# The second branch's gate columns early, as quads of blocks with seven products for eight, and gates kept in DRAM

## The chip, the cores and the metric

One core of a Trainium2 chip runs the program. TensorE (PE) multiplies, VectorE (DVE) and ScalarE (ACT) do elementwise work, GpSimd (POOL) does a few small steps, and SyncE (SP) issues almost all DMAs. The metric is the device time of one execution in microseconds (us), the median of several runs.

## The reference

One layer of an encoder on 256 tokens of 2048 features, all in float32. `w_in` has 8256 columns, the last 4096 of which are the gates of the two branches.

```python
h = rms_norm(x, g_mix)
proj = h @ w_in
c_q, c_kv, k_r, q_d, k_d, v_d, gate = jnp.split(proj, cuts, axis=-1)
...                                  # latent attention -> o_a, dilated attention -> o_b
y_a = o_a.reshape(B, S, MLA_HEADS * V_DIM) @ w_o_mla
y_b = o_b.reshape(B, S, dh) @ w_o_dil
g = jax.nn.sigmoid((gate + b_gate).astype(jnp.float32)).astype(x.dtype)
g = g.reshape(B, S, N_BRANCH, D_MODEL)
x = x + (g[:, :, 0] * y_a + g[:, :, 1] * y_b) @ w_o
gt, up = jnp.split(rms_norm(x, g_ffn) @ w_gate_up, 2, axis=-1)
return x + (jax.nn.silu(gt) * up) @ w_down
```

## The kernel before

**Products in three.** Every float32 operand is split into a rounded high part (a cast on ACT) and the rest (a subtraction on DVE); a product is three products of parts (`mm3`, L426): high by high, high by rest, rest by high. Activations are split once, weights as they stream in. The normalised x stands transposed in SBUF as `xT` (16 row blocks of 128 features by 256 tokens, high `xTh` and rest `xTl`). The division by the root mean square comes after the product, as a factor `rx` per token (`st["x"]`).

**Groups, chunks, steps.** The weight columns are cut into groups (L716 on). An ordinary group has up to 512 columns and accumulates over its row blocks in two banks of PSUM, one for each 128 tokens; its weights come in chunks of two row blocks (512 KB), and a step is the 12 products of a chunk. At the end of a group its `evac` function takes the sums out of PSUM. The groups run in this order: q latents, kv latents, then `g_b` (rotary key, dilated q, k, v) mixed with the up-projections of the latents, the first branch's gates (`evac_g0`, four groups), then the output projections of the two branches, between which the second branch's gates lie (`evac_g1`, four groups), then `w_o`, then the feed-forward part (FFN).

**Quads.** A feed-forward group has 1024 columns, 512 of the gate half and 512 of the other, and takes its 16 row blocks two at a time (`Quad`, L74). Two row blocks, two halves of the columns and two tiles of tokens make a 2x2 by 2x2 block product, which takes eight products of blocks, each over 512 columns. Quads 2, 4 and 6 of eight (`FAST`, L43) take seven products of sums of blocks instead (factors L869); the others are called plain. For these DVE adds weight blocks (L844 to L847) before they are cast and split, and differences of activation blocks are made by DVE (L628 to L631). The seven sums are held in seven PSUM banks, of the tiles mA, mB, sC and sD (`hold_banks`, L127), and are put together by DVE: five steps after the last seven-product quad (`evac_fast`, L658), four after the last plain one (start of `evac_pair`, L670).

**The stream.** SP issues the weight loads in the order of the chunks into three buffers `x` (`xp`, L100); the buffer comes free when its chunk is split. ACT casts and DVE subtracts up to three chunks ahead of PE into six buffers `wh`/`wl` (`wp`, L101). Attention runs as jobs (L431): a step of the main sequence is followed by at most one piece of a job. Loads of biases, residuals and tables are issued a number of steps ahead of a group (`at`, L932). Up to the last two groups ahead of the FFN the program stands in the order in which it is written (`in_order`, L106); after that a scheduler orders it.

**The start.** In the first group the tiles of x come in between the weights. PE transposes them, ACT makes `xTh` (L212), DVE `xTl` (L217). Squares of x are summed on ACT between the steps, and POOL makes `rx` from them.

Of the kernel before, what the change touches and what calls it, by code (L numbers as in the profile page):

```python
# [19 lines left out]
P = 128  # L20
# [21 lines left out]
NPAIR = KD // 2  # L42
FAST = (2, 4, 6)  # L43


# [21 lines left out]
class Group:  # L67
    def __init__(self, w, c0, n, ks, lhs, evac, needs=None, sizes=None):
        self.w, self.c0, self.n, self.ks = w, c0, n, ks
        self.lhs, self.evac, self.needs = lhs, evac, needs or {}  # L70
        self.sizes = sizes


class Quad:  # L74


    def __init__(self, group, i):
        self.group, self.i, self.fast = group, i, i in FAST
        plain = [k for k in range(NPAIR) if k not in FAST]
        self.first, self.last = i == plain[0], i == plain[-1]  # L80
        self.first_fast, self.last_fast = i == FAST[0], i == FAST[-1]

# [12 lines left out]
@with_exitstack  # L95
def layer_kernel(ctx: ExitStack, tc: tile.TileContext, a: dict, out: bass.AP):
    nc = tc.nc
# [141 lines left out]
    def transpose_in(act, k0, nk, src, gname=None):  # L239

        ps = side(f"tr_{act.name}{k0}").rearrange("p (k s) -> p k s", s=S)
        for k in range(nk):
            for t in range(NT):
                nc.tensor.transpose(ps[:, k, t * P:(t + 1) * P], src(t, k0 + k), ident)
        h, l = act.tiles(k0 // 4)
        o = k0 % 4
        if gname is None:
            split_evac((h[:, o:o + nk], l[:, o:o + nk], ps[:, :nk], None))
        else:
            split_evac(*((h[:, o + k], l[:, o + k], ps[:, k], gain(gname, k0 + k)) for k in range(nk)))  # L250

    xT = Act("xT", KD)

    def job_x(k0, nk):
        transpose_in(xT, k0, nk, lambda t, k: xn[k // 4][:, t, (k % 4) * P:(k % 4 + 1) * P], "g_mix")
        return
        yield

    xjobs, xjob_of = [], {}
# [292 lines left out]
    for p in range(4):  # L552
        attn["mla", p] = Job(job_attn("mla", p), [prep["kr"], gains])
        attn["dil", p] = Job(job_attn("dil", p), [prep["qd"], prep["kd"], bdone["vd"]])


    g0, tj, mT, gbias = {}, {}, Act("mT", KD), {}
# [14 lines left out]
    def evac_g0(j):  # L572
        def evac(ps, step):
            g0[j] = gate_evac(ps, j, f"g0_{j}")
        return evac

    def evac_ya(j):
        def evac(ps, step):
            nc.scalar.activation(g0[j], g0[j], AF.Sigmoid)
            nc.vector.tensor_mul(g0[j], ps, g0[j])  # L580
        return evac

    def evac_g1(j):
        def evac(ps, step):
            tj[j] = gate_evac(ps, 4 + j, f"g1_{j}")
            nc.scalar.activation(tj[j], tj[j], AF.Sigmoid)
        return evac
# [25 lines left out]
    def job_h(i):  # L613
# [7 lines left out]
        if i not in FAST:  # L621
            hP[i] = t4([P, 2, 2, S], f"hP{i}", F32R)
            split_evac(*((hP[i][:, 0, k], hP[i][:, 1, k], ps[:, k], g[k]) for k in range(2)))
        else:
            v, l, h = t4([P, 8, P], f"hs{i}"), t4([P, 7, P], f"hsl{i}", F32R), t4([P, 7, P], f"hsh{i}", F32R)
            nc.scalar.activation(v[:, 0:8:7], ps[:, 0].rearrange("p (t s) -> p t s", t=NT), AF.Copy, scale=g[0])
            nc.scalar.activation(v[:, 1:3], ps[:, 1].rearrange("p (t s) -> p t s", t=NT), AF.Copy, scale=g[1])
            nc.vector.tensor_sub(v[:, 3], v[:, 7], v[:, 2])  # L628
            nc.vector.tensor_sub(v[:, 4], v[:, 7], v[:, 0])
            nc.vector.tensor_sub(v[:, 5], v[:, 0], v[:, 3])  # L630
            nc.vector.tensor_sub(v[:, 6], v[:, 1], v[:, 5])  # L631
            split_pair(h, l, v[:, :7])
            hq[i] = (h, l)
        return
# [22 lines left out]

    def evac_fast(q):  # L658

        bank, z, u = held["q"], t4([P, NT, 512], f"z{q.group.c0}"), t4([P, NT, 512], f"u{q.group.c0}")  # L660
        add, sub = nc.vector.tensor_add, nc.vector.tensor_sub
        with tc.high_priority(offset=PRIO):
            nc.scalar.copy(u[:, 0], bank[1])
            sub(z[:, 0], bank[6], u[:, 0])
            add(u[:, 1], bank[7], z[:, 0])
            add(z[:, 1], bank[5], u[:, 1])
            add(z[:, 0], bank[5], z[:, 0])
        q.group.zu = z, u

    def evac_pair(half, i, last):  # L670

        def evac(zu, step):
            q = held["q"]
            z, u = zu
            add, sub = nc.vector.tensor_add, nc.vector.tensor_sub
            with tc.high_priority(offset=PRIO):
                add(z[:, 1], q[0], z[:, 1])
                add(z[:, 0], q[3], z[:, 0])
                add(u[:, 0], q[2], u[:, 0])  # L679
                sub(u[:, 1], q[4], u[:, 1])  # L680
            r = st["2"]
# [42 lines left out]

    g_in(0, 512, evac_lat("cq"), sizes=[1, 1])
    g_in(512, 512, evac_lat("ckv"))
# [6 lines left out]
    g_b(6)  # L733
    for j in range(4):
        g_in(OFF_GATE + 512 * j, 512, evac_g0(j))
# [84 lines left out]
    def load(c):  # L820
        g, gi, ks, q = chunks[c]
        t = xt[c] = xp.tile([P, 4, 512], F32, name=f"x{c}", tag="x")
        if q:
            for kk in range(2):
                src = g.w[(2 * q.i + kk) * P:(2 * q.i + kk + 1) * P].rearrange("p (n f) -> p n f", n=2)
                nc.sync.dma_start(t[:, 2 * kk:2 * kk + 2], src[:, :, g.c0:g.c0 + 512])
            return
# [22 lines left out]
    def split(c):  # L850
# [4 lines left out]
        h = w8(f"wh{c}")  # L855
        h, l = (h, w8(f"wl{c}")) if gi >= ffn_at else (h[:, :2], h[:, 2:])
        s = (slice(None), slice(0, 4 if q else len(ks)), slice(0, 512 if q else g.n))
# [14 lines left out]
    def products_quad(c):  # L872
        q = chunks[c][3]
        bank, w = held["q"], parts.pop(c)
        if not q.fast:
            h, l = w
            for t, n in ((1, 0), (0, 0), (0, 1), (1, 1)):
                m = PLAIN[t, n]
                for kk in range(2):
                    s = slice(t * P, (t + 1) * P)  # L880
                    mm3(bank[m], hP[q.i][:, 0, kk, s], hP[q.i][:, 1, kk, s], h[:, 2 * kk + n], l[:, 2 * kk + n],
                        q.first and kk == 0, q.last and kk == 1)
        else:
            h, l = hq[q.i]
            for m in (1, 6, 7, 5, 3, 2, 4):
# [89 lines left out]
    splits(2)  # L975
    jobs.extend((gains, xstat))
    gains.ready = 8
    xstat.ready = 2
    for i, (c, ks, first, last) in enumerate(steps):
        g, gi, allks, q = chunks[c]  # L980
        if first and gi == ffn_at - 2:
            in_order.close()
        for fn in early.get(i, ()):
            fn()
# [11 lines left out]
        if gi == ffn_at and not held:  # L996
            hold_banks()
        ps = products(i)
        if last and gi < len(groups) - 1:
# [60 lines left out]
```

## Time and profile before

| | |
|---|---|
| median of three runs | 1356.53 us (1354.4, 1356.53, 1360.9) |
| the profiled execution | 1356.11 us, span from first to last instruction 1354.3 us, granted clock 1.000 |
| PE, DVE, ACT, POOL busy | 99%, 70%, 48%, 3% of the span |
| DMA | 257.14 MB, mean 190 GB/s |
| gate groups of the second branch | between the output projections; the first output projection starts at 367 us, the last gate of the four is taken out of PSUM at 522 us |
| feed-forward part | from 634.7 us to the end |

A row of a group of instructions gives line, engine, operation, output<-inputs, shapes and count, then total busy us and mean ns of one, then the idle time of the engine ahead of them and what ended it. A row of a timeline starts with its start and duration in us; in square brackets stands an idle time before it. A row of a window gives the stretch and its length, then the busy us of PE, weight loads, DVE, ACT and POOL with their counts, the PE clock, the busy share of the DMA engines and GB/s. A row of waits gives who waited for whom: total us, times, longest. Matmuls overlap in the records, so their duration is longer than the distance of their starts; the distance is what a product costs.

### The profile page before, as it was taken

To read this page: it belongs to the slowest core of one execution; us is meant where nothing else is said; L and a number is where in the kernel's file an instruction comes from. 1 tells how busy PE (TensorE), PEld (TensorE's weight loads), DVE (VectorE), ACT (ScalarE), POOL (GpSimd) and SP (SyncE) were. 2 spreads that over 40 slices of the span, in tenths; PEclk is the share of its full clock that TensorE was granted. 3 is DMA by queue.
4 is the path that set the end of the run, shared out by engine and by line. 5 is a ranking of instruction groups with operands and counts; after the bars stand their busy time and mean duration, and the time that the engine had idled before them with its cause. 6 is when DMAs were issued, how large, how long until landed. Compare 5 with 4: busy or idle time off the path is not lost.

```text
span 1354.3 us, 16169 instructions
## 1 busy us (share of the span) xinstructions
PE 1339.5 (99%) x6243; PEld 1126.0 (83%) x6243; DVE 949.1 (70%) x949; ACT 652.2 (48%) x724; POOL 34.3 (3%) x41
## 2 busy tenths in 40 slices
PE   8999999999999999999999999999999999999998
PEld 6899999988888888888788888888878888888886
DVE  5566777677645655567789756886798579857973
ACT  6455555454444444455455434454445345534541
POOL 1011112000000000000000000000000000000000
PEclk9999999999999999999999999999999999999999
DMA  7555555656556766676546665565457654754662
GB/s 247 179 175 161 161 170 167 184 161 176 174 186 205 212 188 202 209 235 207 201 158 213 221 187 183 191 213 190 157 185 245 191 186 172 229 190 163 214 214 93
DMA packets 138205, 257.14 MB, mean 190 GB/s; under 512 B 9192, under 2 KB 28688, under 8 KB 138128
## 3 DMA queue, kind: packets, MB, share of 16 engines
q1 hardware_dynamic: 137760, 255.96, 58.9%
q8 instruction: 49, 0.80, 0.2%
q14 instruction: 28, 0.23, 0.1%
q10 hardware_dynamic: 144, 0.13, 0.0%
q0 software_dynamic: 224, 0.01, 0.0%
HBM read 253.97 MB, written 2.10 MB: 189 GB/s over the span
## 4 chain that ended last, share of the span: by engine, by line
PE 94%; DVE 2%; issue 1%; DMA 1%; ACT 1%; SPq 0%; DVEq 0%; ACTq 0%
PE g L429 14%; PE g L427 14%; PE g L428 13%; PE sC L427 6%; PE sC L429 6%; PE sC L428 6%; PE mA L427 4%; PE mA L429 4%; PE mA L428 4%; PE sD L429 4%; PE sD L427 4%; PE sD L428 4%; PE mB L428 3%; PE mB L429 3%; PE mB L427 3%
## 5 line engine op out<-in xcount | busy, mean ns | idle before, releaser
L220 ACT CAST wh<-x 128x1024 fp32r<-128x1024 f32 (+3 forms) x349 | 465.3, 1352 | 437.0 <-DVE x L847 127.7
L221 DVE TENSOR_TENSOR wl<-x,wh 128x2048 fp32r<-128x2048 f32 x132 | 300.8, 2289 | 134.5 <-ACT wh L220 132.7
L221 DVE TENSOR_TENSOR wh<-x,wh 128x1024 fp32r<-128x1024 f32 (+2 forms) x217 | 250.6, 1172 | 113.1 <-ACT wh L220 111.9
L427 PE MATMUL g<-wh,xTh 128*128 128x512 f32 (+1 forms) x544 | 210.6, 387 | 0.6 <-ACT xTh L212 0.6
L429 PE MATMUL g<-wh,xTl 128*128 128x512 f32 (+1 forms) x544 | 207.9, 382 | 0.6 <-DVE xTl L217 0.6
L428 PE MATMUL g<-wh,xTh 128*128 128x512 f32 (+1 forms) x544 | 207.9, 382 | 0.0
L429 PEld LDWEIGHTS g<-wh,xTl 128*128 128x128 f32 x544 | 102.8, 189 | 17.6 <-DVE xTl L217 1.4
L427 PEld LDWEIGHTS g<-wh,xTh 128*128 128x128 f32 x544 | 102.8, 189 | 15.9 <-ACT xTh L212 0.9
L428 PEld LDWEIGHTS g<-wh,xTh 128*128 128x128 f32 x544 | 102.9, 189 | 15.4 <-DVE wh L221 0.4
L427 PE MATMUL sC<-wh,hP 128*128 128x512 f32 x220 | 86.1, 391 | 1.6 <-DVE u L679 1.5
L429 PE MATMUL sC<-wh,hP 128*128 128x512 f32 x220 | 85.7, 390 | 0.0
L429 PE MATMUL sD<-wh,hP 128*128 128x512 f32 x220 | 85.7, 389 | 0.0
L428 PE MATMUL sC<-wl,hP 128*128 128x512 f32 x220 | 85.7, 389 | 0.0
L427 PE MATMUL sD<-wh,hP 128*128 128x512 f32 x220 | 85.7, 389 | 0.0
L428 PE MATMUL sD<-wl,hP 128*128 128x512 f32 x220 | 85.7, 389 | 0.0
L220 ACT CAST rh<-x 128x1024 fp32r<-128x1024 f32 x33 | 34.7, 1051 | 36.1 <-DMA x<-in_w_gate_up_dram 36.1
L427 PEld LDWEIGHTS sC<-wh,hP 128*128 128x128 f32 x220 | 41.3, 188 | 12.3 <-issue 4.0
L427 PE MATMUL g<-wh,mTh 128*128 128x512 f32 x128 | 50.5, 394 | 0.0
L429 PE MATMUL g<-wh,mTl 128*128 128x512 f32 x128 | 49.9, 390 | 0.0
L428 PE MATMUL g<-wh,mTh 128*128 128x512 f32 x128 | 49.9, 390 | 0.0
L427 PEld LDWEIGHTS sD<-wh,hP 128*128 128x128 f32 x220 | 41.3, 188 | 8.6
L428 PEld LDWEIGHTS sD<-wl,hP 128*128 128x128 f32 x220 | 41.3, 188 | 8.6
(675 smaller groups left out, 2390.7 us busy)
## 6 DMA issues: line engine op xcount, KB each, us to landing
x<-in_w_gate_up_dram SPq DMA_DIRECT2D x176, 512.0 KB, 4.7
x<-in_w_down_dram SPq DMA_DIRECT2D x88, 512.0 KB, 5.0
x<-in_w_in_dram SPq DMA_DIRECT2D x79, 512.0 KB, 4.2
x<-in_w_in_dram SPq DMA_DIRECT2D x56, 448.0 KB, 3.6
x<-in_w_o_dram SPq DMA_DIRECT2D x32, 512.0 KB, 4.4
x<-in_w_o_mla_dram SPq DMA_DIRECT2D x16, 512.0 KB, 4.9
x<-in_w_o_dil_dram SPq DMA_DIRECT2D x16, 512.0 KB, 4.6
x<-in_w_ukv_dram SPq DMA_DIRECT2D x8, 512.0 KB, 4.0
```

The source lines that it names most:

```text
L220: nc.scalar.copy(h, x)
L221: nc.vector.tensor_sub(l, x, f32(h))
L427: nc.tensor.matmul(ps, ah, bh, start=first, stop=False)
L428: nc.tensor.matmul(ps, ah, bl, start=False, stop=False)
L429: nc.tensor.matmul(ps, al, bh, start=False, stop=last)
```

## The change

The 2048 gate columns of the second branch become two groups of 1024, computed as quads on `xT`, five plain and three of seven products each (`FAST_X`). They run third and fourth in the program, behind the first two gate groups of the first branch, which are now first and second. The quads of x are made in the first group: ACT copies each block out of PSUM a second time (`copy_blocks`), DVE makes the differences and splits them (`sums_of`) before the quads begin. These gate values, and the raw values of gates 0 and 1, are stored in a DRAM tensor (six tiles of 512 KB) and loaded again eight steps ahead of the output projection that they multiply. The output projections now follow each other without gate groups between them. The second to fourth groups are ordered by the scheduler; from the fifth on the written order holds as before. Two loads of biases move to the start of the program.

```diff
+FAST_X = (2, 4, 6)
...
     def job_x(k0, nk):
-        transpose_in(xT, k0, nk, lambda t, k: xn[k // 4][:, t, (k % 4) * P:(k % 4 + 1) * P], "g_mix")
+        ps = transpose_in(xT, k0, nk, lambda t, k: xn[k // 4][:, t, (k % 4) * P:(k % 4 + 1) * P], "g_mix")
+        if nk == 2 and k0 // 2 in FAST_X:
+            xv[k0 // 2] = v = t4([P, 8, P], f"xv{k0}")
+            copy_blocks(v, ps, [gain("g_mix", k0 + k) for k in range(2)])
...
+    def combine(zu):
+
+        q = held["q"]
+        z, u = zu
+        add, sub = nc.vector.tensor_add, nc.vector.tensor_sub
+        with tc.high_priority(offset=PRIO):
+            add(z[:, 1], q[0], z[:, 1])
+            add(z[:, 0], q[3], z[:, 0])
+            add(u[:, 0], q[2], u[:, 0])
+            sub(u[:, 1], q[4], u[:, 1])
...
     def evac_g0(j):
         def evac(ps, step):
+            xstat.finish(step)
             g0[j] = gate_evac(ps, j, f"g0_{j}")
+            if j < 2:
+                nc.sync.dma_start(gd[j], g0[j])
+        return evac
+
+    def load_gate(j, to, k):
+        to[k] = t4([P, NT, 512], f"gd{j}")
+        nc.sync.dma_start(to[k], gd[j])
+
+    def evac_gates(j):
+
+        def evac(zu, step):
+            combine(zu)
+            for e in range(2):
+                for t in range(NT):
+                    nc.vector.scalar_tensor_tensor(zu[e][:, t], zu[e][:, t], st["x"][:, t:t + 1], gbias[4 + j + e],
+                                                   op0=ALU.mult, op1=ALU.add)
+                nc.scalar.activation(zu[e], zu[e], AF.Sigmoid)
+                nc.sync.dma_start(gd[2 + j + e], zu[e])
         return evac
...
-    g_in(0, 512, evac_lat("cq"), sizes=[1, 1])
+    g_in(OFF_GATE + 512 * 0, 512, evac_g0(0), sizes=[1, 1])
+    g_in(OFF_GATE + 512 * 1, 512, evac_g0(1))
+    for j in (0, 2):
+        groups.append(Group(W["w_in"], OFF_GATE + 2048 + 512 * j, 1024, range(NPAIR), xT, evac_gates(j),
+                            {k: (lambda k=k: [xqjob[k]]) for k in FAST_X}, fast=FAST_X))
+    g_in(0, 512, evac_lat("cq"))
     g_in(512, 512, evac_lat("ckv"))
...
-    for j in range(4):
+    for j in range(2, 4):
         g_in(OFF_GATE + 512 * j, 512, evac_g0(j))
...
     for j in range(4):
         out_mla(j)
-        g_in(OFF_GATE + 2048 + 512 * j, 512, evac_g1(j))
-        if j:
-            out_dil(j - 1)
-    out_dil(3)
+    for j in range(4):
+        out_dil(j)
...
     for j in range(4):
-        at(gidx("evac_g0", j), lambda j=j: load_bias(j))
-        at(gidx("evac_g1", j), lambda j=j: load_bias(4 + j))
+        at(gidx("evac_g0", j), lambda j=j: load_bias(j), 0 if j < 2 else 8)
+        at(gidx("evac_gates", j // 2), lambda j=j: load_bias(4 + j), -2)
+        at(gidx("evac_yb", j), lambda j=j: load_gate(2 + j, tj, j))
+    for j in range(2):
+        at(gidx("evac_ya", j), lambda j=j: load_gate(j, g0, j))
...
-        if first and gi == ffn_at - 2:
+        if first and gi in (1, ffn_at - 2):
             in_order.close()
+        if first and gi == 4:
+            in_order.enter_context(tc.manual_schedule())
```

Lines of the changed kernel are numbered anew in what follows. The start of the program on SP before: `xn` are tiles of x, the other loads are the weights of chunks 1 to 3.

```order
L835 DMA x_106<-in_w_in_dram 128x512
L168 DMA xn_89<-in_x_dram 128x2x256
L835 DMA x_109<-in_w_in_dram 128x2x512
L168 DMA xn_90<-in_x_dram 128x2x256
L835 DMA x_130<-in_w_in_dram 128x2x512
```

The same place now:

```order
L884 DMA x_106<-in_w_in_dram 128x512
L169 DMA xn_89<-in_x_dram 128x2x256
L884 DMA x_109<-in_w_in_dram 128x2x512
L616 DMA bias_130<-in_b_gate_dram 128x512
L616 DMA bias_400<-in_b_gate_dram 128x512
L169 DMA xn_90<-in_x_dram 128x2x256
L884 DMA x_132<-in_w_in_dram 128x2x512
```

The two bias loads stand between the weights of chunk 2 and the x tile and weights of chunk 3.

On DVE the end of a gate group of the second branch before: one instruction pair takes the gate out of PSUM (L569), with weight splits (L221) on both sides.

```order
L221 TENSOR_TENSOR wh_3937<-x_3906,wh_3937 128x1024
L221 TENSOR_TENSOR wh_3954<-x_3923,wh_3954 128x1024
L569 SCALAR_TENSOR_TENSOR g_2_3971<-g_3839,rx,bias_3677 128x512 x2
L221 TENSOR_TENSOR wh_3977<-x_3940,wh_3977 128x1024
L221 TENSOR_TENSOR wh_3995<-x_3957,wh_3995 128x1024
```

The end of the first of the two gate groups now: L595 is the last step after the seven-product quads, L604 to L607 are the four of `combine`, L643 the bias steps, and L894 to L896 with `x_769` are the sums of weight blocks of the next group's first seven-product quad; the last row is the split of a raw block of the seven-product quad after that.

```order
L595 TENSOR_TENSOR z_835<-mB,z_835 128x512
L604 TENSOR_TENSOR z_835<-sD,z_835 128x512
L605 TENSOR_TENSOR z_835<-sC,z_835 128x512
L606 TENSOR_TENSOR u_836<-sC,u_836 128x512
L607 TENSOR_TENSOR u_836<-sD,u_836 128x512
L894 TENSOR_TENSOR x_769<-x_769 128x512
L643 SCALAR_TENSOR_TENSOR z_835<-z_835,rx,bias_663 128x512
L895 TENSOR_TENSOR x_769<-x_769 128x512
L643 SCALAR_TENSOR_TENSOR z_835<-z_835,rx,bias_663 128x512
L896 TENSOR_TENSOR x_769<-x_769 128x512
L643 SCALAR_TENSOR_TENSOR u_836<-u_836,rx,bias_665 128x512 x2
L222 TENSOR_TENSOR rl_886<-x_846,rh_885 128x1024
```

The four bias steps stand between the block sums of the next group, ahead of the split of the summed blocks.

More of the change, by code (lines that the diff above doesn't have):

```diff
@@ L67, with __init__ @@
 class Group:
-    def __init__(self, w, c0, n, ks, lhs, evac, needs=None, sizes=None):
+    def __init__(self, w, c0, n, ks, lhs, evac, needs=None, sizes=None, fast=FAST):
         self.w, self.c0, self.n, self.ks = w, c0, n, ks
         self.lhs, self.evac, self.needs = lhs, evac, needs or {}
-        self.sizes = sizes
+        self.sizes, self.fast = sizes, fast
 class Quad:
     def __init__(self, group, i):
-        self.group, self.i, self.fast = group, i, i in FAST
-        plain = [k for k in range(NPAIR) if k not in FAST]
+        self.group, self.i, self.fast = group, i, i in group.fast
+        plain = [k for k in range(NPAIR) if k not in group.fast]
         self.first, self.last = i == plain[0], i == plain[-1]
-        self.first_fast, self.last_fast = i == FAST[0], i == FAST[-1]
+        self.first_fast, self.last_fast = i == group.fast[0], i == group.fast[-1]
 class Flag:
@@ L95, in layer_kernel @@
 @with_exitstack
-def layer_kernel(ctx: ExitStack, tc: tile.TileContext, a: dict, out: bass.AP):
+def layer_kernel(ctx: ExitStack, tc: tile.TileContext, a: dict, out: bass.AP, gd: bass.AP):
     nc = tc.nc
@@ L656, in layer_kernel @@
     sg, hidT, djobs = {}, {}, {}
[L658 to L668, printed above, removed]
     def evac_pair(half, i, last):
         def evac(zu, step):
-            q = held["q"]
             z, u = zu
[L675 to L680, printed above, removed]
+            combine(zu)
             r = st["2"]
@@ L880, in products_quad @@
                     s = slice(t * P, (t + 1) * P)
[L881 removed]
+                    if q.group.lhs:
+                        ah, al = q.group.lhs(2 * q.i + kk)
+                    else:
+                        ah, al = hP[q.i][:, 0, kk], hP[q.i][:, 1, kk]
+                    mm3(bank[m], ah[:, s], al[:, s], h[:, 2 * kk + n], l[:, 2 * kk + n],
                         q.first and kk == 0, q.last and kk == 1)
         else:
[L884 removed]
+            h, l = (xq if q.group.lhs else hq)[q.i]
             for m in (1, 6, 7, 5, 3, 2, 4):
@@ L976, in layer_kernel @@
     jobs.extend((gains, xstat))
+    jobs.extend(xqjob.values())
+    for j in xqjob.values():
+        j.ready = 9
     gains.ready = 8
@@ L995, in layer_kernel @@
             loads(ahead_of + 2)
-        if gi == ffn_at and not held:
+        if q and not held:
             hold_banks()
+        elif held and gi < ffn_at and not q:
+            held.clear()
+            spare.clear()
         ps = products(i)
```

60 lines of the change are left out of this document (42 added, 18 removed).

## The prediction

> **What bounds the kernel now.** I read the page first: the busy times and the chain that ended last.
>
> ```profile
> span 1354.3 us, 16169 instructions
> PE 1339.5 (99%) x6243; PEld 1126.0 (83%) x6243; DVE 949.1 (70%) x949; ACT 652.2 (48%) x724; POOL 34.3 (3%) x41
> ...
> PE 94%; DVE 2%; issue 1%; DMA 1%; ACT 1%; SPq 0%; DVEq 0%; ACTq 0%
> ```
>
> TensorE is busy for 99% of the span and is 94% of the chain. That a PE is busy need not mean that it runs at its own pace, so I went to the waits of PE, and then to its timeline in a plain quad of the feed-forward part (24 products, the last followed by transposes).
>
> ```profile
> PE pg L174 <- DMA gmix_rows<-in_g_mix_dram: 2.6, 1, 2.6
> PE tr_xT L244 <- DMA xn<-in_x_dram: 1.8, 3, 0.8
> PE sD L691 <- DVE z L685: 1.7, 2, 1.0
> PE sC L427 <- DVE u L679: 1.5, 5, 0.9
> PE g L427 <- ACT xTh L212: 0.6, 1, 0.6
> PE g L429 <- DVE xTl L217: 0.6, 1, 0.6
> ```
>
> ```profile
> 727.28 0.39 PE L427 MATMUL sD<-wh,hP 128*128 128x512 f32 x1
> ...
> 732.50 0.40 PE L429 MATMUL sD<-wh,hP 128*128 128x512 f32 x1
> 732.73 1.03 PE L691 MATMUL mA<-ident,z 128*128 128x128 f32 x8
> ```
>
> These waits of PE come to 8.8 us in 1354, and all lie at the start or in the feed-forward part; none is in the projections and gates between. The 24 products start over 732.73 - 727.28 = 5.45 us, 0.227 us each. So the time of this kernel is the number of PE's products times 0.227 us, plus the start and a few seams. A change can bring what it takes off that number, and can lose what it adds in waits.
>
> **The products.** In 512-column groups, 1024 gate columns take 2 x 16 row blocks x 2 token tiles x 3 products = 192. In quads, five plain ones take 24 each and three seven-product ones 7 x 3 = 21: 183. Nine fewer, twice: 18 x 0.227 = **4.1 us less**. The gate columns moved are otherwise the same weights in the same bytes. The attention jobs keep their distances in steps, since they start from the kv and value groups and not from the gates: the last of them now lie beside output projections instead of gates, at 12 products a step as before. The feed-forward part keeps its order on every engine. The rotary tables' four small loads and their four products on DVE only move back with the groups they belong to.
>
> **The start.** The first group is now gate 0, and its two bias loads (256 KB each) stand in SP's order behind the load of chunk 2, ahead of the second x tile and of chunk 3. Here is the place in the profile: SP's issues, then ACT, then PE, then the DMA rate.
>
> ```profile
> 3.61 0.47 SPq L835 DMA_DIRECT2D x<-in_w_in_dram  x1
> 4.12 0.47 SPq L168 DMA_DIRECT2D xn<-in_x_dram  x1
> 6.02 0.37 SPq L835 DMA_DIRECT2D x<-in_w_in_dram  x1
> ```
>
> ```profile
> 10.22 1.04 ACT L220 CAST wh<-x 128x1024 fp32r<-128x1024 f32 x1 [2.80 <-DMA x<-in_w_in_dram]
> 12.21 1.05 ACT L220 CAST wh<-x 128x1024 fp32r<-128x1024 f32 x1 [0.95 <-DMA x<-in_w_in_dram]
> 13.16 0.83 ACT L212 ACTIVATE xTh<-tr_xT,gmix 128x256 fp32r<-128x256 f32 x2
> ```
>
> ```profile
> 11.48 0.63 PE L428 MATMUL g<-wh,xTh 128*128 128x512 f32 x1
> 11.91 0.63 PE L429 MATMUL g<-wh,xTl 128*128 128x512 f32 x1
> 12.34 0.70 PE L244 MATMUL tr_xT<-ident,xn 128*128 128x128 f32 x4
> 13.68 0.50 PE L427 MATMUL g<-wh,xTh 128*128 128x512 f32 x1 [0.65 <-ACT xTh L212]
> 14.02 0.39 PE L428 MATMUL g<-wh,xTh 128*128 128x512 f32 x1
> 14.96 0.50 PE L429 MATMUL g<-wh,xTl 128*128 128x512 f32 x1 [0.56 <-DVE xTl L217]
> 15.30 0.39 PE L427 MATMUL g<-wh,xTh 128*128 128x512 f32 x1
> 15.53 0.39 PE L428 MATMUL g<-wh,xTh 128*128 128x512 f32 x1
> ```
>
> ```profile
> 9.00:12.00 3.00, 3.00 (x10) 2.51 (x11) 0.70 (x1) 1.04 (x1) 0.00 (x0) 1.00 1.05 372
> 12.00:15.00 3.00, 1.80 (x9) 0.93 (x7) 2.23 (x4) 2.55 (x4) 0.00 (x0) 1.00 0.90 282
> ```
>
> ACT casts chunk 3 at 12.21, the moment it lands, and only then makes the xTh that PE waits for at 13.68. DMA is full there (share 1.05 and 0.90). The two loads put 0.524 MB before chunk 3: at 372 GB/s 1.4 us, at 282 GB/s 1.9 us. Lower end 0, if the queue lets chunk 3 pass; upper end 1.9 plus two issues of 0.47 on SP, 2.8. I take **1.4 us**, since 372 GB/s is the rate of the stretch in which chunk 3 waits its turn. The wait for xTl at 14.96 moves along and costs nothing more.
>
> ACT also copies six blocks of x in this group (0.83 us for each of three tiles, what two xTh of that size take). The first pair falls into ACT's wait for chunk 5's weights, the others into the slack that the later start of PE leaves. Nought; if that cover were gone, 0.83 us once for each tile, 2.5 in all.
>
> PE's own pace changes in these rows: 11.91 - 11.48 = 0.43 us a product, 0.23 from 15.30 on. The idle before 13.68 grows from 0.65 to about 2 us. If this kept PE slow for the 12 products of chunk 2, it would cost 12 x 0.20 = 2.4 us more. [...]
>
> The sums of those blocks, 3 x (four of 128x128 and a split of 128x896), come on DVE: with the row below and the 1.22 of a split of 128x1024 (next fence), at most 3 x (1.1 + 1.2) = 7 us. They fall under gate 0 and gate 1; gate 1's eight weight splits of that size take 9.8 of its 21.8 us. Nought; the first of them is needed only 11 us into the quads.
>
> ```profile
> 620.09 0.28 DVE L629 TENSOR_TENSOR hs<-hs 128x128 f32<-128x128 f32 x1
> ```
>
> **The quads.** Each gate group of 1024 columns gets the work that a feed-forward group has today, so its rows price it.
>
> ```profile
> L221 DVE TENSOR_TENSOR wl<-x,wh 128x2048 fp32r<-128x2048 f32 x132 | 300.8, 2289 | 134.5 <-ACT wh L220 132.7 <-PE g L429 1.0
> L221 DVE TENSOR_TENSOR rl<-x,rh 128x1024 fp32r<-128x1024 f32 x33 | 40.2, 1220 | 5.7 <-ACT rh L220 5.4
> L845 DVE TENSOR_TENSOR x<-x 128x512 f32<-128x512 f32 x33 | 22.8, 691 | 0.9
> L569 DVE SCALAR_TENSOR_TENSOR g<-g,rx,bias 128x512 f32<-128x512 f32 x16 | 11.3, 746 | 17.3 <-PE g L429 17.3
> L678 DVE TENSOR_TENSOR z<-sC,z 128x512 f32<-128x512 f32 x11 | 7.5, 683 | 0.0
> ```
>
> ```profile
> 708.11 4.49 DVE L221 TENSOR_TENSOR wl<-x,wh 128x2048 fp32r<-128x2048 f32 x2 [2.05 <-ACT wh L220]
> ...
> 678.00:721.00 43.00, 42.89 (x193) 35.10 (x193) 38.51 (x39) 23.82 (x19) 0.00 (x0) 1.00 0.57 196
> ```
>
> DVE per group: 5 plain quads x 2.29 = 11.4; 3 seven-product ones x (1.22 + 5 x 0.69 for what is 128x512 + 2.29) = 20.9; eight sums out of PSUM x 0.68 and four bias steps x 0.75 = 8.4. Sum 40.7 us, against 183 x 0.227 = 41.5 us of PE. The feed-forward group measured here (678 to 721) carries the same but for two bias steps less and one 1.22 us split of hidden values more; its DVE is busy 38.5 us, because neighbouring instructions overlap a little, and PE loses almost nothing (42.89 of 43.00). So I cost the inside of a gate group at nothing. The cover is the two or three quads that are split ahead; without it see the first rival.
>
> Between the two gate groups PE waits for a sum out of the bank that it writes first, as at the seam L427 <- L679: 1.5 us in five, longest 0.9. **0.3 us** for the one seam, between 0 and 0.9. From gate 1 into the first quads there is no such wait (those banks held only transposes), nor out of the second gate group: the two banks that the next 512-column groups take are emptied a whole plain quad (5.4 us) earlier.
>
> **Queues that are passed.** Six stores and six loads of 512 KB are new on SP. A store waits there for the gate's last step on DVE or ACT, and weight loads are queued behind it. After the first gate group that is four bias steps (3.0 us on DVE) and on ACT two sigmoids of 128x1024 (by the cast of that size 1.04 us each) with a table load. But the next weight load needs the buffer of a seven-product quad whose split stands behind those bias steps in DVE's order, so it could not start sooner, and its quad comes after three plain quads and two of seven products, 3 x 5.45 + 2 x 4.8 = 26 us of PE. Nought; without that cover the 5 us and the table load would be paid once. The six reads are 3 MB over the 87 us of the output projections (32 steps of 12 products), and DMA has room there:
>
> ```profile
> 450.00:510.00 60.00, 60.00 (x270) 49.77 (x270) 34.81 (x30) 27.70 (x28) 0.00 (x0) 1.00 0.66 200
> ```
>
> Each is asked for eight steps (22 us) ahead of its use. Nought; a late one would cost, at the 200 GB/s of that row, the 2.6 us of its 512 KB.
>
> **Sum.** The profiled execution took 1356.11 us with a span of 1354.3. 1356.1 - 4.1 + 1.4 + 0.3 = 1353.7. The median of the runs shown is 0.4 above that execution, so **1354.0 us** is the forecast.
>
> **The rivals.**
>
> *DVE becomes the bound of the gate groups (slower).* At 708.11 DVE stands idle for 2.05 us: the summed blocks must be cast by ACT before they can be split. Three such gaps a group, if nothing fills them, make 40.7 + 6.2 = 46.9 us of DVE against 41.5: 5.4 us a group, 10.8 for two, 1364.5 us. For it: DVE has 0.8 us to spare by the nominal sum, so it starts to cost once more than 0.8 us of the 6.2 is unfilled. Against it: the feed-forward groups have the same gaps and PE runs through. Half of it, 3.1 us a group unfilled, gives 40.7 + 3.1 - 41.5 = 2.3 us a group and 1358.6 us.
>
> *The clock stays low in the start.* 2.4 us more, 1356.4 us; with chunk 3 slow as well 1358.8.
>
> *The start absorbs the loads.* Then only the products and the seam count: 1352.6 us.
>
> *A real gain, over 6.8 us.* The products give 4.1 at most, and the gate groups that are replaced have no waits to lose; the rest would have to come out of the start, where the change only adds.
>
> **How the numbers follow.** Half a per cent, 6.8 us, is about what a measurement of this kernel can tell from no change (its own three runs spread over 6.5). The forecast has 0.60, the absorbed start 0.12, the low clock or half of the DVE rival 0.17, the full DVE rival 0.08, a real gain 0.03. The forecast's own span is 1351 to 1356; 8 in 10 needs the half-way cases too: 1350.5 to 1360. Faster by over 0.5% is 0.04, slower 0.09 (the full rival, and a noisy median), within it 0.87.
>
> **What would show it.** Right: 18 fewer products on PE; the first product of chunk 2 near 15 instead of 13.68, waiting for xTh, with chunk 3's landing ended later by the bias loads; PE at 0.227 us through both gate groups, with one wait under 1 us between them; no PE wait in the output projections. Wrong: PE waiting for wl or wh inside a gate group, SP issuing a weight load late behind a store, or an output projection waiting for a gate tile.

## The result and the profile after

| | time, us | to the kernel before |
|---|---|---|
| forecast | 1354.0 (1350.5 to 1360.0) | within half a per cent |
| before, six runs beside the changed kernel | median 1358.3 (1354.4 to 1360.9) | 1 |
| changed, six runs | median 1365.2 (1363.16 to 1368.81) | 1.0054, 95% 1.0040 to 1.0068 |
| changed, the profiled execution | 1363.27, span 1361.5 | span before: 1354.3 |

The changed kernel is slower by half a per cent, 7 us, and outside the range. From its page: the span, PE's busy time, and the chain of work that ended last.

```profile
span 1361.5 us, 16195 instructions
...
PE 1338.9 (98%) x6225; PEld 1123.4 (83%) x6225; DVE 989.4 (73%) x1000; ACT 669.9 (49%) x735; POOL 34.3 (3%) x41
...
PE 86%; DVE 5%; DMA 3%; ACT 2%; issue 2%; SPq 0%; DVEq 0%; POOL 0%; ACTq 0%
```

PE makes 6225 products and transposes in place of 6243: the 18 are gone, as forecast. But the span is 7.2 us longer, and PE is busy for only 0.6 us less of it: it stands idle for 7.8 us more. The shares of the chain do not measure this: PE's fall from 94% to 86% would be some 100 us. PE's waits, by total, number and longest:

```profile
PE sC L457 <- DVE u L606: 4.2, 6, 3.5
PE tr_xT L245 <- DMA xn<-in_x_dram: 3.9, 3, 1.9
PE pg L175 <- DMA gmix_rows<-in_g_mix_dram: 2.4, 1, 2.4
PE g L457 <- ACT xTh L213: 2.1, 1, 2.1
PE mA L457 <- DVE z L592: 1.5, 1, 1.5
PE mA L685 <- ACT hs L257: 1.4, 1, 1.4
PE mla0pt L547 <- DVE mla0p L540: 1.2, 1, 1.2
```

Against before, `tr_xT` has 2.1 us more and `xTh` 1.5 more, both in the start. The second is not the change's doing: e5 below, whose start is that of the kernel before, waits 2.1 us for `xTh` as well. In the profile of before the clock was full from 12.54 us on, in the changed kernel's from 9.43 (products 0.43 us apart ahead of it, 0.23 behind it); a PE that is faster earlier comes to the same wait earlier. In e3 and e4, whose bias loads come later, products stand 0.23 us apart from 10.64 and from 9.56 on, and the wait is 1.60 and 2.13 us. The waits for `u` (longest 3.5, before 0.9) and for `z` L592 lie at the seam between the two gate groups, and the one for `mla0p` at the first softmax.

A list of waits leaves out what PE loses while it works at half its clock (products 0.43 us apart in place of 0.23, granted clock 0.50 from 108.41 to 115.24 us). So I took for each product the distance to the next start, less its usual distance (0.227 us for 512 columns, the median for other shapes), and added up what is left over in each stretch of the profiled executions. The last three columns belong to experiments below.

| lost by PE, us | before | changed | look-ahead (e2) | and biases (e3) | and sigmoid (e4) |
|---|---|---|---|---|---|
| start, 0 to 40 us | 8.8 | 11.7 | 11.2 | 9.4 | 10.4 |
| gate 1 and first gate quads, 40 to 100 | 0.1 | 1.4 | 2.6 | 1.8 | 1.0 |
| seam of the gate groups, 100 to 115 | 0.0 | 8.1 | 1.3 | 1.3 | 1.2 |
| to the first softmax, 115 to 265 | 0.5 | 1.8 | 3.5 | 3.1 | 0.4 |
| attention, output projections, 265 to 620 | 0.2 | 0.8 | 0.8 | 0.8 | 0.8 |
| into the feed-forward part, 620 to 700 | 2.0 | 2.4 | 7.2 | 2.9 | 3.0 |
| rest of the feed-forward part | 6.4 | 3.5 | 3.3 | 3.8 | 3.5 |
| sum | 18.0 | 29.5 | 29.9 | 23.1 | 20.4 |

The changed kernel loses 11.5 us more; less 4.1 us of products that is 7.4, and the spans differ by 7.2. So the account is complete: the seam carries most of it, then the start, then small pieces.

**The start.** SP, ACT and PE in the changed kernel (start, duration, idle before):

```profile
4.12 0.94 SPq L616 DMA_DIRECT2D bias<-in_b_gate_dram  x2
```

```profile
14.26 1.04 ACT L221 CAST wh<-x 128x1024 fp32r<-128x1024 f32 x1 [2.41 <-DMA x<-in_w_in_dram]
15.21 0.83 ACT L213 ACTIVATE xTh<-tr_xT,gmix 128x256 fp32r<-128x256 f32 x2
```

```profile
12.96 0.63 PE L245 MATMUL tr_xT<-ident,xn 128*128 128x128 f32 x4 [1.92 <-DMA xn<-in_x_dram]
15.73 0.50 PE L457 MATMUL g<-wh,xTh 128*128 128x512 f32 x1 [2.14 <-ACT xTh L213]
...
17.60 0.63 PE L457 MATMUL g<-wh,xTh 128*128 128x512 f32 x1
18.03 0.63 PE L458 MATMUL g<-wh,xTh 128*128 128x512 f32 x1
```

The cast of chunk 3 starts at 14.26 (12.21 before) and the first product of chunk 2 at 15.73 (13.68 before): 2.05 us for the two loads. Then the products start 0.43 us apart (18.03 - 17.60) and not 0.23: the granted clock had been full since 9.4 us and fell to half (0.50) at 16.25, for 3.41 us.

**The seam.** ACT, DVE and PE where the first gate group ends (PE's last product of it starts at 103.81), then windows with PE's clock as the third number from the end:

```profile
99.48 1.91 ACT L221 CAST wh<-x 128x2048 fp32r<-128x2048 f32 x1 [3.63 <-DMA x<-in_w_in_dram]
102.72 1.05 ACT L221 CAST rh<-x 128x1024 fp32r<-128x1024 f32 x1 [1.32 <-DMA x<-in_w_in_dram]
103.68 0.61 ACT L221 CAST r<-x 128x512 fp32r<-128x512 f32 x1
104.19 0.58 ACT L591 COPY u<-mA 128x512 f32<-128x512 f32 x1
```

```profile
101.43 2.29 DVE L222 TENSOR_TENSOR wl<-x,wh 128x2048 fp32r<-128x2048 f32 x1 [2.46 <-ACT wh L221]
103.81 1.23 DVE L222 TENSOR_TENSOR rl<-x,rh 128x1024 fp32r<-128x1024 f32 x1
104.95 0.68 DVE L592 TENSOR_TENSOR z<-mA,u 128x512 f32<-128x512 f32 x1
...
109.74 0.68 DVE L606 TENSOR_TENSOR u<-sC,u 128x512 f32<-128x512 f32 x1
```

```profile
103.81 0.39 PE L459 MATMUL sD<-wh,xTl 128*128 128x512 f32 x1
105.69 0.50 PE L457 MATMUL mA<-r,hshx 128*128 128x512 f32 x1 [1.48 <-DVE z L592]
...
110.47 0.80 PE L457 MATMUL sC<-wh,xTh 128*128 128x512 f32 x1 [3.46 <-DVE u L606]
...
112.52 0.63 PE L457 MATMUL sD<-wh,xTh 128*128 128x512 f32 x1
```

```profile
100.00:105.00 5.00, 4.20 (x19) 3.16 (x17) 3.49 (x3) 3.45 (x4) 0.00 (x0) 1.00 0.96 328
105.00:110.00 5.00, 1.23 (x3) 0.48 (x3) 5.00 (x10) 1.47 (x2) 0.00 (x0) 0.84 0.52 201
110.00:115.30 5.30, 4.83 (x11) 3.69 (x12) 5.30 (x9) 2.58 (x3) 0.00 (x0) 0.51 0.07 26
```

The seven-product sums in mA and mB were complete by 96.7 us (the last product into mB starts at 96.33 and takes 0.39). `evac_fast` (L591 to L595) could have started then. It starts at 104.19, because on ACT and on DVE the split of the next group's second quad and the splits of raw blocks of its third stand ahead of it, and their weights land late: ACT waits 3.63 us for one and 1.32 for the other. Everything after that is a chain of 0.68 us steps on DVE, and PE stands for 1.48 and 3.46 us. The clock is then at half (0.50) from 108.41 to 115.24, with products 0.43 us apart, and PE is busy for 4.77 us of it; by my estimate the 2.4 us that this costs make up most of the rest of the 8.1.

What SP waited for between 80 and 120 us shows why the weights are late:

```profile
SPq L875 <- DVE wl L222: 23.0, 7, 8.1
SPq L616 <- DVE z L643: 9.0, 1, 9.0
```

The weight loads wait for a buffer `x`, that is for the DVE split of the chunk that holds it, 23 us in seven waits. The 9.0 us are a load of the next group's biases. It stands behind the last of those weight loads (issued by 104.6 us), so it did not make them late; the next weight load goes out at 118.84, and PE waits for no weights after it.

By my estimate the depth of the look-ahead alone would have held `evac_fast` up for most of that time. `ahead_of` (L1055) is the first chunk that is not split yet, so c + 4 means three chunks ahead of the one on PE, and c + 3 two (the expectations below count PE's own chunk too, as four and three). A chunk of 512 columns takes one of the six buffers `wh`/`wl`, a quad takes two (L905). Six hold PE's quad and two more, so a third one ahead has to wait until PE is through with a quad. Here PE began the last quad of the group, and so was done with the one before, at 98.60; the weights came at 99.48. Weights in time would have brought `evac_fast` forward by some 2 us (0.9 for the one split and 1.32 for the other), out of the 7.5 between 96.7 and 104.19.

**The first softmax.** ACT and PE:

```profile
253.70 1.28 ACT L536 ACT_TABLE_LOAD   x1
```

```profile
260.62 0.63 PE L547 MATMUL mla0pt<-ident,mla0p 128*128 128x128 f32 x4 [1.21 <-DVE mla0p L540]
```

Before, the table for the exp was loaded at 0.72 us and no other before 374.67, behind the first softmaxes. Now the gates' sigmoids load another one at 109.57 (1.28 us), and the exp loads its own again, at 253.70.

### The profile page after: what moved, and what is told of

Its sections match the earlier page's. It is cut to its first block, busy times and chain, and to the rows that moved or that the text cites. A ratio compares the mean times of both kernels' runs of the same rounds, so it can differ in the third digit from the quotient of the medians.

```text
span 1361.5 us, 16195 instructions
## 1 busy us (share of the span) xinstructions
PE 1338.9 (98%) x6225; PEld 1123.4 (83%) x6225; DVE 989.4 (73%) x1000; ACT 669.9 (49%) x735; POOL 34.3 (3%) x41
## 4 chain that ended last, share of the span: by engine, by line
PE 86%; DVE 5%; DMA 3%; ACT 2%; issue 2%; SPq 0%; DVEq 0%; POOL 0%; ACTq 0%
PE g L459 10%; PE g L457 10%; PE g L458 10%; PE sC L457 6%; PE sC L459 6%; PE sC L458 6%; PE mA L457 4%; PE mA L459 4%; PE mA L458 4%; PE sD L457 4%; PE sD L459 4%; PE sD L458 4%; PE mB L458 3%; PE mB L459 3%; PE mB L457 3%
## 5 line engine op out<-in xcount | busy, mean ns | idle before, releaser
L221 ACT CAST wh<-x 128x2048 fp32r<-128x2048 f32 (+3 forms) x333 | 462.9, 1408 | 446.4 <-DVE x L896 158.4
L222 DVE TENSOR_TENSOR wl<-x,wh 128x2048 fp32r<-128x2048 f32 x148 | 337.2, 2289 | 149.2 <-ACT wh L221 147.5
L222 DVE TENSOR_TENSOR wh<-x,wh 128x1024 fp32r<-128x1024 f32 (+3 forms) x185 | 212.5, 1163 | 80.4 <-ACT wh L221 79.5
L457 PE MATMUL g<-wh,xTh 128*128 128x448 f32 (+1 forms) x416 | 160.3, 385 | 2.1 <-ACT xTh L213 2.1
L459 PE MATMUL g<-wh,xTl 128*128 128x448 f32 (+1 forms) x416 | 158.1, 380 | 0.5 <-DVE xTl L218 0.5
L458 PE MATMUL g<-wh,xTh 128*128 128x448 f32 (+1 forms) x416 | 157.9, 380 | 0.0
L457 PEld LDWEIGHTS g<-wh,xTh 128*128 128x128 f32 x416 | 78.8, 189 | 12.7 <-ACT xTh L213 2.4
L459 PEld LDWEIGHTS g<-wh,xTl 128*128 128x128 f32 x416 | 78.8, 189 | 12.3 <-DVE xTl L218 1.0
L458 PEld LDWEIGHTS g<-wh,xTh 128*128 128x128 f32 x416 | 78.8, 189 | 10.8 <-DVE wh L222 0.4
L221 ACT CAST rh<-x 128x1024 fp32r<-128x1024 f32 x39 | 41.0, 1050 | 44.2 <-DMA x<-in_w_gate_up_dram 33.0
L222 DVE TENSOR_TENSOR rl<-x,rh 128x1024 fp32r<-128x1024 f32 x39 | 47.5, 1219 | 6.4 <-ACT rh L221 6.0
L457 PEld LDWEIGHTS sC<-wh,hP 128*128 128x128 f32 x220 | 41.3, 188 | 11.6 <-issue 3.2
L459 PEld LDWEIGHTS sC<-wh,hP 128*128 128x128 f32 x220 | 41.3, 188 | 8.6
```

The lines of the kernel that those rows point to most:

```text
L221: nc.scalar.copy(h, x)
L222: nc.vector.tensor_sub(l, x, f32(h))
L457: nc.tensor.matmul(ps, ah, bh, start=first, stop=False)
L458: nc.tensor.matmul(ps, ah, bl, start=False, stop=False)
L459: nc.tensor.matmul(ps, al, bh, start=False, stop=last)
```

## The experiments

The theory: three separate losses, in the order in which the account shows them. At the seam, the gate quads are split one chunk deeper (`ahead_of` gives c + 4 ahead of the feed-forward part but for the last group, c + 3 in its quads), which puts splits of late weights ahead of `evac_fast` on ACT and DVE, which took them in the order written (ACT stood idle for 1.32 us ahead of the cast at 102.72, with the sums for `evac_fast` complete since 96.7). In the start, the bias loads. At the first softmax, the table. Rivals: DVE has too much to do in the gate groups (the first rival of the prediction, priced at 1364.5 us, all but what was measured); the stores hold up SP; the sigmoids hold up ACT at the seam.

Each kernel was timed against the kernel before on the same chip (medians 1358.7 us for e1 to e4, 1357.4 for e5 to e8, 1358.8 for e9 and e10); the ratios compare them.

**e1: bias loads later.**

```diff
-        at(gidx("evac_g0", j), lambda j=j: load_bias(j), 0 if j < 2 else 8)
+        at(gidx("evac_g0", j), lambda j=j: load_bias(j), (-5 if j < 1 else 4) if j < 2 else 8)
```

> The two bias loads are issued in the second half of the first group, everything else stays. Theory (three separate losses: start 3.2 us, seam between the gate groups 8.0, first exp 1.4): the start is given back, so about 3 us less than the changed kernel, 1362; in the trace chunk 3 lands near 12.2 us, the first product of chunk 2 starts near 13.7 and the granted clock does not fall back near 16; the seam stays. Rival (the bias loads only use up slack in the start, the loss is all in the gate groups): no change, 1365, and the seam 3 us longer.

Measured: 1363.45 us, ratio 1.0036 (1.0022 to 1.0051), 2.4 us less than the change's 1.0054; the two intervals overlap, so the times alone do not prove a gain. In the trace the cast of chunk 3 and the first product of chunk 2 come back to where they were, 2 us earlier (12.20 and 13.67). But PE was slow behind it all the same: the product that starts at 14.95 us takes 0.77 us in the records, against 0.50 at the same place before (14.96) and 0.79 at half clock in the changed kernel (17.01). So the fall of the clock does not hang on the bias loads alone; of e3 and e4, which have them as late as e1, e4 has products 0.43 us apart there and e3 has not (rows at e8). The seam still loses 8.0.

**e2: the look-ahead of the feed-forward quads.**

```diff
-            ahead_of = c + AHEAD + 1 + (gi < ffn_at - 1)
+            ahead_of = c + AHEAD + 1 + (gi < ffn_at - 1 and not q)
```

> The splits in the gate quads run three chunks ahead of PE, as in the feed-forward part, instead of four; the same work on every engine. Theory (splits of weights that land late stand ahead of evac_fast on ACT and DVE): evac_fast starts 5 us or more earlier, the seam falls from 8.0 us lost to 1 or 2 and the clock stays full there; 1358.5 to 1359.5 in all. Rival (DVE has too much work in the gate groups): nothing is taken off DVE, so the gate groups last as long, 1365. Rival (SP's stores and bias loads hold up the weight loads): SP's order is the same, 1365.

Measured: 1360.28 us, ratio 1.0014 (1.0003 to 1.0025), 5.4 us less than the change. DVE and PE at the seam (PE's last product of the group starts at 104.68):

```profile
99.74 0.68 DVE L592 TENSOR_TENSOR z<-mA,u 128x512 f32<-128x512 f32 x1
...
102.48 2.29 DVE L222 TENSOR_TENSOR wl<-x,wh 128x2048 fp32r<-128x2048 f32 x1
104.69 0.68 DVE L605 TENSOR_TENSOR z<-sC,z 128x512 f32<-128x512 f32 x1
105.29 0.68 DVE L606 TENSOR_TENSOR u<-sC,u 128x512 f32<-128x512 f32 x1
```

```profile
106.12 0.47 PE L457 MATMUL sC<-wh,xTh 128*128 128x512 f32 x1 [1.05 <-DVE u L606]
```

L592 starts at 99.74 in place of 104.95, the split of the late weights stands behind it, and one wait of 1.05 us is left, a little above the longest (0.9) of the feed-forward seams before. DVE's work is the same, 989.4 us of it. The seam was the order. Its profiled execution lost 4.8 us more than the change's where the feed-forward part begins (a wait of 3.8 us for `hs`, and a clock of 0.8 in the slice of its page from 647 to 681 us, 0.9 or more in every other), which is why the account's sum hardly moves while the timed runs do.

**e3: both.** The edits of e1 and e2 together, nothing else.

> Both edits together. Theory: the two losses are independent, 1365.2 - 3 - 6.5 = 1355.5, some 3 us below the kernel before; PE loses under 2 us at the seam and under 9 in the first 40 us. Rival (DVE bound): 1362 at best, from the start alone.

Measured: 1357.92 us, ratio 0.9992 (0.9980 to 1.0005), 8.4 us less than the change; the two losses add up. That is level with the kernel before, and 2.4 us short of what was expected.

**e4: and the sigmoid after the reload.** On top of e3.

```diff
-                nc.scalar.activation(zu[e], zu[e], AF.Sigmoid)
...
+            nc.scalar.activation(tj[j], tj[j], AF.Sigmoid)
             nc.vector.tensor_mul(tj[j], ps, tj[j])
```

> As the run with both edits, and the sigmoid of the second branch's gates is taken after they are loaded again, so that no table load stands between the gate groups and the first exp. Theory: another 1.4 us, 1354; PE's wait for the first exp near 259 us is gone. Rival (that wait comes from DVE or ACT work and not from the table load): it stays, 1355.5.

Measured: 1355.52 us, ratio 0.9973 (0.9963 to 0.9983): below both kernels, by 3.2 us and by some 11 us. Against e3 the intervals just touch. The wait for `mla0p` is gone, and so is a loss of about 1 us near 177 us that e2 and e3 had.

**e5: the deeper look-ahead put into the kernel before.** The doubled test of the seam: nothing of the gates in it.

```diff
-            ahead_of = c + AHEAD + 1 + (gi < ffn_at - 1)
+            ahead_of = c + AHEAD + 1 + (gi < ffn_at - 1 or q is not None)
```

> The kernel before, with one edit: its feed-forward quads are split four chunks ahead, as the gate quads of the changed kernel are. No gates are moved. Theory (the deeper look-ahead puts splits of late weights ahead of the sums out of PSUM): each of the six seams between two quad groups of the feed-forward part loses what the seam of the gate groups lost, 5 to 8 us in place of 0.9 or less, so 1358 + 25 to 45 = 1383 to 1403 us. Rival (the seam is long because of the gate groups' own work, bias steps, sigmoids and stores, or DVE's load there): nothing of that is in the feed-forward part, 1358.

Measured: 1397.87 us, ratio 1.0288 (1.0259 to 1.0317), 40 us more, 6.7 for each of the six seams. PE's first row of waits, and DVE and PE at one seam:

```profile
PE sC L427 <- DVE u L679: 31.3, 6, 7.2
```

```profile
677.91 2.29 DVE L221 TENSOR_TENSOR wl<-x,wh 128x2048 fp32r<-128x2048 f32 x1 [2.47 <-ACT wh L220]
680.12 1.22 DVE L221 TENSOR_TENSOR rl<-x,rh 128x1024 fp32r<-128x1024 f32 x1
681.25 0.68 DVE L664 TENSOR_TENSOR z<-mA,u 128x512 f32<-128x512 f32 x1
```

```profile
686.87 0.77 PE L427 MATMUL sC<-wh,hP 128*128 128x512 f32 x1 [5.28 <-DVE u L679]
```

The same three rows as at the seam of the gates: a split that came late, the split of a raw block, and only then `evac_fast`. Why the first one came late differs. Its cast on ACT shows it:

```profile
675.96 1.91 ACT L220 CAST wh<-x 128x2048 fp32r<-128x2048 f32 x1 [2.85 <-PE sD L428]
```

It waited for PE, which frees the buffer `wh`, and not for weights. So it is at four of the six seams; at two the cast waits for weights, and at five the raw blocks' cast does, for 0.3 to 2.2 us. The run confirms the order, in a place without any of the gates' work. That weights are late is only part of it: one chunk more does not fit into the six buffers. PE's waits for `u` went from 1.5 us in five to 31.3 in six; by my estimate the clock makes up most of the rest: its mean went from 1.000 to 0.985, some 21 us of the span, a part of it inside the waits, and at the seam shown products start 0.23 us apart ahead of the wait and 0.43 behind it (688.82 and 689.25).

**e6: the stores on POOL's queue.**

```diff
-                nc.sync.dma_start(gd[j], g0[j])
+                nc.gpsimd.dma_start(gd[j], g0[j])
...
-                nc.sync.dma_start(gd[2 + j + e], zu[e])
+                nc.gpsimd.dma_start(gd[2 + j + e], zu[e])
```

> The changed kernel with its six stores on POOL's queue in place of SP's. Rival (weight loads are queued behind stores on SP, and land late for that): SP goes on past the stores, the seam shrinks and it is 1358 to 1362. Theory: the late loads wait for a buffer and not for a store, so the seam between the gate groups stays at 8 us and the time at 1365.

Measured: 1366.55 us, ratio 1.0066 (1.0046 to 1.0086); the seam loses 8.6 us. The stores were not what the weights waited for.

**e7: the gates early, without quads.** Otherwise e4; the loads of these gates' biases move with the groups, and the scheduled stretch ends behind the four groups.

```diff
-    for j in (0, 2):
-        groups.append(Group(W["w_in"], OFF_GATE + 2048 + 512 * j, 1024, range(NPAIR), xT, evac_gates(j),
+    for j in range(4):
+        g_in(OFF_GATE + 2048 + 512 * j, 512, evac_g1(j))
...
+    def evac_g1(j):
+        def evac(ps, step):
+            g = gate_evac(ps, 4 + j, f"g1_{j}")
+            nc.sync.dma_start(gd[2 + j], g)
```

> As the run with all three edits (bias loads late, sigmoid late), but the early gates of the second branch are computed as four ordinary groups of 512 columns: 18 products more, no sums, no seam of quads; gates still early and kept in DRAM. Theory (the gain is the products, and moving the gates and keeping them in DRAM costs nothing): 1355.5 + 4.1 of products - 1.2 of seam - 0.6 of the wait inside the quads = 1357.8. Rival (part of the gain of that run comes from output projections that follow each other without gates between them): 1355 to 1356.

Measured: 1359.78 us, ratio 1.0011 (0.9998 to 1.0024), 5.2 us above e4 where 2.3 were expected. PE loses nothing between 40 and 115 us. So moving the gates and keeping them in DRAM costs nothing that these runs can tell, and it gains nothing either: what e4 gains comes with the quads. Of the 5.2 us, 4.1 are the products. In the profiles the feed-forward part differs more than the total: this kernel loses 12.7 us there (4.8 and 7.9) and e4 6.5, though the code is the same; why, I did not settle.

**e8: PE kept busy in the start.** e4 with 16 transposes more, whose results nobody reads.

```diff
+        if i == 2:
+            for m in range(16):
+                nc.tensor.transpose(warm[:, 0, :P], ident, ident)
```

> As the run with all three edits, and PE makes 16 transposes of the identity (about 1.8 us, results unused) in the start, where it waits for the xTh of chunk 2. [...]

The run asks whether PE, kept busy in the start, keeps its full clock there, and whether the time follows. e3 and e4 have the same start, and PE's pace differs in it. PE in e3, then in e4:

```profile
13.76 0.50 PE L457 MATMUL g<-wh,xTh 128*128 128x512 f32 x1 [1.60 <-ACT xTh L213]
...
17.44 0.60 PE L245 MATMUL tr_xT<-ident,xn 128*128 128x128 f32 x4
```

```profile
13.70 0.50 PE L457 MATMUL g<-wh,xTh 128*128 128x512 f32 x1 [2.13 <-ACT xTh L213]
...
18.84 0.73 PE L245 MATMUL tr_xT<-ident,xn 128*128 128x128 f32 x4
```

Chunk 2 begins within 0.06 us, and ends 1.4 us apart: in e4 its products start 0.43 us apart from 15.85 us on, in e3 0.23. With the transposes (e8):

```profile
10.97 1.91 PE L1057 MATMUL warm<-ident 128*128 128x128 f32 x16
13.18 0.50 PE L457 MATMUL g<-wh,xTh 128*128 128x512 f32 x1 [0.30 <-ACT xTh L213]
...
72.11 0.50 PE L458 MATMUL mA<-wl,hshx 128*128 128x512 f32 x1 [1.54 <-DVE wl L222]
```

The profile's mean clock is 1.000, against 0.999 in e4; 3.41 us at half, as in the changed kernel's start, would take 0.0013 off, so by this estimate none such is in it. But e3 has 1.000 too, without the transposes, so this one profile does not prove that they did it. The time did not follow: 1357.13 us, ratio 0.9994 (0.9983 to 1.0005), more than e4 and not less. PE is 1.2 us ahead of e4 at 70 us and 0.2 us behind it at 72, after a wait for `wl` that e4 does not have: PE reaches the first seven-product gate quad earlier, its split does not come earlier. In e3 the 0.9 us that it is ahead of e4 are gone at the same place. So in these three profiles the fall of the clock in the start cost nothing in the end. The profiled execution of e8 then loses 4.2 us more than e4's from 620 us on, where the code is that of e4; between the ratios it is some 2.9. That is left open.

**e9: less work for DVE.**

```diff
-FAST_X = (2, 4, 6)
+FAST_X = (2, 6)
```

> The changed kernel with two seven-product quads a gate group in place of three: DVE has 4.7 us less to do in each gate group (6.97 for a seven-product quad, 2.29 for a plain one), PE three products (0.7 us) more. Rival (DVE is the bound of the gate groups): both groups get shorter by what DVE has less, up to 8 us in all, 1357 to 1360. Theory (the order on DVE and ACT at the seam): splits of late weights still stand ahead of the sums out of PSUM, the seam still loses 6 to 8 us, and with the extra products it is 1365 to 1367.

Measured: 1367.19 us, ratio 1.0067 (1.0052 to 1.0083). The first gate group but its ends, in the changed kernel and in e9 (the third busy time is DVE's):

```profile
64.00:105.00 41.00, 39.73 (x173) 31.93 (x171) 32.73 (x30) 19.87 (x15) 0.00 (x0) 1.00 0.67 231
```

```profile
64.00:105.00 41.00, 39.73 (x176) 32.56 (x174) 28.43 (x23) 19.90 (x14) 0.00 (x0) 1.00 0.64 227
```

DVE has 4.3 us less to do and the seam still loses 8.4. With three seven-product quads DVE is idle for 8 us in this stretch as well: its load is not the bound. What counts is the order of its work.

**e10: only the sigmoid after the reload.** The edit of e4 in the changed kernel.

> The changed kernel with the sigmoid of the second branch's gates taken after they are loaded again, nothing else. Theory: PE's wait of 1.4 us at the first exp is gone, since no table has to be loaded there, and the seam stays: 1363.8. Rival (the sigmoids on ACT at the seam are what holds the seam up, by a table load of 1.28 us and two operations of 1 us): the seam falls from 8 to 4 or less, 1359 to 1360.

Measured: 1364.52 us, ratio 1.0049 (1.0032 to 1.0066). The 0.7 us to the change's ratio are within the intervals; in the trace the wait for `mla0p` is gone and the seam loses 7.8. The sigmoids do not hold the seam up.

## Why the prediction was wrong

**The products** were right: 18 fewer, 4.1 us.

**The seam between the gate groups** is the step that failed: "Between the two gate groups PE waits for a sum out of the bank that it writes first, as at the seam L427 <- L679 ... 0.3 us for the one seam, between 0 and 0.9." It took 8.1 us. The price was read from feed-forward seams, where two quads are split ahead of PE's. The line that sets this gives three ahead of the feed-forward part, and the change puts quads there for the first time. "The cover is the two or three quads that are split ahead" left open which of the two, and it mattered. The timeline on DVE has the splits (101.43 and 103.81) above `evac_fast`; the rows of the order that I had quoted begin at its last step, L595. I counted DVE's work in the group (40.7 of 41.5 us) and did not ask what stands ahead of the one piece for which PE waits, nor when its data land. With the shallower look-ahead (e2 to e4, e8) the seam cost 1.2 to 1.3, still above the 0.9.

**The start** was right in its mechanism and too small: 2.05 us for the loads against 1.4, inside its bounds of 0 to 2.8, and about 1 us more when the clock falls (2.9 in the account, e4 to e3 1.0). That fall was the rival "the clock stays low in the start", at 2.4 us; it occurred, at under half of that price. "The idle before 13.68 grows from 0.65 to about 2 us" came true (2.14), but by luck: e5, without the loads, has 2.1 and e4 2.13. The forecast has no term for the fall: that a wait of 2 us would leave the clock full was my assumption, and the trace of before does not show it. In the changed kernel PE stood for 2.14 us at a stretch and was busy for 0.34 of the 3.41 us from 12.84 to 16.25, and the clock fell at their end.

**Costed at nothing, and not nothing:** the new table load at the first softmax, 1.2 us of wait in the profile, and waits for `wl` inside the gate quads, 0.4 us in the changed kernel and up to 1.6 in the experiments.

**Costed at nothing, and right:** the stores and loads on SP, the copies and sums of x, the output projections (0.6 us more lost from 265 to 620 us, none of it in a wait), the end of the second gate group. No output projection waits for a gate tile.

**The rival "DVE becomes the bound of the gate groups"** came out at the right time, 1364.5 us, for a wrong reason: that is luck. (It adds 10.8 us to 1353.7, where the other rivals start from 1354.0.) Its signs (DVE idle for want of a cast, PE waiting for DVE) could be read into the profile after; only taking work off DVE (e9) and changing the order alone (e2) told them apart. Of the prediction's signs of being right, "PE at 0.227 us through both gate groups, with one wait under 1 us between them" failed; of its signs of being wrong, PE's wait for `wl` inside a gate group came, at 0.4 us.

## What to carry to other kernels

When a piece of work is moved to another place in a program, its price in the old place holds only if what orders it there holds as well: read the look-ahead of the new place, and the rows on each engine that stand ahead of the step for which the busiest engine waits. A deeper look-ahead was no safer here: a split that had to wait, for its weights (3.63 us at the seam of the gates) or for a buffer (2.85 at the one of e5), held up the finished work behind it, and 40 us of e5 came from one chunk more. Count the buffers that a deeper look-ahead needs. At the seam PE's waits were paid for twice, once as 4.94 us of idleness (1.48 and 3.46) and once as 6.83 us at half the clock.

## What the runs showed of the hardware

In the changed kernel's profile the granted clock was full from 9.43 us, half (0.50) from 16.25 to 19.66, full to 108.41, half (0.50) to 115.24, and full from there to 1361.1, 0.4 us ahead of the end. In the profile of before it was full from 12.54 us to 0.4 us ahead of the end. At full clock products over 512 columns started 0.23 us apart, at half 0.43. In the 3.41 us ahead of the changed kernel's two falls PE had been busy for 0.34 (12.84 to 16.25) and 0.36 (105.00 to 108.41) of the time; its longer idle stretches in the second were 0.69 and 1.40 us. With the same start, PE waited for `xTh` for 2.13 us in e4 and for 1.60 in e3; the products of chunk 2 behind it came to stand 0.43 us apart in e4 and stayed at 0.23 in e3, and the chunk ended 1.4 us later in e4. Busy shares go by modelled ends of the products, so they are rough. What sets the moment of a fall, these runs do not show.
